# RMSNorm on one core: nineteen transfers of x and out joined into twelve, with whole-tile loads of the second and third tile

## The chip, the core and the metric

The kernel runs on one core of a Trainium2 chip. The metric is device time in microseconds (us) of one execution. The core has a matmul engine (TensorE, PE), three engines that matter here, VectorE (DVE), ScalarE (ACT) and GpSimd (POOL), and SyncE (SP), which in this kernel issues all transfers. The transfers themselves are carried out by 16 DMA engines.

## The reference

```python
batch, seq, dim = 16, 1024, 512          # x: float32, gamma: float32 [512]
eps = 1e-5
rms = np.sqrt(np.mean(x ** 2, axis=-1, keepdims=True) + eps)
return (x / rms * gamma).astype(np.float32)
```

x has 16,384 rows of 512 numbers, 33.55 MB, and out has as many. Every row is divided by its own root mean square and multiplied by gamma.

## The kernel before, in words

**Tiles and slots.** The rows are cut into four tiles of 128 partitions x 32 rows: partition p of a tile holds 32 rows that follow each other in memory, 64 KB. Three buffers, slot0 to slot2, hold tiles 0, 1 and 2, and tile 3 goes into slot0 once tile 0 has been stored. Everything is done in place: a slot is loaded, scaled and stored. A transfer names a range of rows, so that `load(0, 0, 8, 16)` brings rows 8 to 15 of tile 0 into slot0, for all 128 partitions (lines 44 to 50).

**Groups.** Compute runs over nine groups (lines 76 to 86). A group is (tile, first row, number of rows, pieces, share). For each group:
- `square_sums` (lines 89 to 99) goes over the pieces: ScalarE squares the rows of a piece into a scratch (line 96), VectorE sums each row (line 97). The scratch is PSUM for the first and third piece and a buffer for the second; a piece of 9 rows uses rows 23 to 31 of slot2 as its scratch, so these rows of slot2 can only be loaded once the last such piece has been summed.
- `inverse_rms` (lines 101 to 104): ScalarE takes the square root (line 102), VectorE the reciprocal (line 103).
- `scale_by_pool` (lines 106 to 113): GpSimd multiplies the last `share` rows by the reciprocal (line 109) and by gamma (line 110).
- `scale` (lines 115 to 118): ScalarE multiplies the other rows by the reciprocal, a row at a time (line 118), and `times_gamma` (line 122) lets VectorE multiply them by gamma, which stands in PSUM for it.

**Order.** The order on each engine is the order in which the program is written; nothing rearranges it. The main loop (from line 166) interleaves two groups: it issues the GpSimd part of group k, the squares of group k+1 (at most two pieces), half of ScalarE's scaling of group k, the third piece of squares of group k+1 if there is one, the rest of the scaling, VectorE's gamma product of group k, then the transfers that follow group k, and last the square root and reciprocal of group k+1. Engines run each through its own list and wait where they need another's result.

**Transfers.** SP issues all of them in program order. Those ahead of the loop (lines 52 to 61) are the first loads and gamma, which comes in pieces of a part of its 512 numbers; the others are issued by `transfers` (lines 129 to 149) after certain groups. An instruction of SP that waits holds up all that stand behind it. What the waits are: a load into a slot waits for the stores that read it and for compute that used it as scratch; a store waits for VectorE's and GpSimd's last product on its rows. There are also eight completion semaphores, taken in turn, so that the k-th transfer waits for the one eight before it.

In this text L0a and L0b are the loads of the first and second half of tile 0, L1, L2 those of tiles 1 and 2, L3a and L3b those of tile 3's halves; S0a, S0b, S1, S2, S3a and S3b are the stores.

Of the kernel before, what the change touches and what calls it, by code (L numbers as in the profile page):

```python
# [9 lines left out]
def kernel(  # L10
# [15 lines left out]
    N, D = xf.shape  # L26
# [17 lines left out]
    def load(t, slot, r0, r1):  # L44
        dma = nc.sync.dma_start(out=slots[slot][:, r0:r1], in_=xv[t][:, r0:r1])  # L45
        before_scale.append((slot, r0, r1, dma))

    def store(t, slot, r0, r1):
        dma = nc.sync.dma_start(out=ov[t][:, r0:r1], in_=slots[slot][:, r0:r1])
        before_scale.append((slot, r0, r1, dma))  # L50

    gamma_row = const.tile([1, D], fp32)
    pieces = (0, 128, 224, 320, 416, D)

    load(0, 0, 0, 1)
    load(0, 0, 1, 8)
    for c0, c1 in zip(pieces, pieces[1:]):
        nc.sync.dma_start(out=gamma_row[:, c0:c1], in_=gamma.unsqueeze(0)[:, c0:c1])
    load(0, 0, 8, 16)
    load(0, 0, 16, 32)  # L60
    load(1, 1, 0, 16)

    ones_col = const.tile([1, P], fp32)
    nc.gpsimd.memset(ones_col, 1.0)  # L64
# [9 lines left out]


    groups = [
        (0, 0, 7, (7,), 3),
        (0, 7, 9, (9,), 5),
        (0, 16, 16, (7, 9), 7),
        (1, 0, 16, (7, 9), 7),  # L80
        (1, 16, 16, (7, 5, 4), 7),
        (2, 0, 16, (7, 5, 4), 7),
        (2, 16, 16, (7, 5, 4), 7),
# [44 lines left out]

    def transfers(t, g):
        if (t, g) == (0, 0):  # L130
            store(0, 0, 0, 1)
            load(1, 1, 16, 32)
            store(0, 0, 1, 2)
            load(2, 2, 0, 23)
        elif (t, g) == (0, 16):
            store(0, 0, 2, 3)
            load(2, 2, 23, 32)
            store(0, 0, 3, 16)
            store(0, 0, 16, 32)
            load(3, 0, 0, 16)  # L140
            load(3, 0, 16, 32)
        elif (t, g) == (1, 16):
            store(1, 1, 0, 32)
        elif (t, g) == (2, 16):
            store(2, 2, 0, 32)
        elif (t, g) == (3, 0):
            store(3, 0, 0, 16)
        elif (t, g) == (3, 16):
            store(3, 0, 16, 32)
# [16 lines left out]
    for k, group in enumerate(groups):  # L166
        t, g, n, pieces, share = group
        mine = n - share
        half = (mine + 1) // 2
        ahead = groups[k + 1 :][:1]  # L170
        ss, todo = pieces_of(ahead[0]) if ahead else (None, [])
        scale_by_pool(rstd, t, g, n, share)
        for piece in todo[:2]:
            square_sums(*piece)
        scale(rstd, t, g, 0, half)
        for piece in todo[2:]:
            square_sums(*piece)
        scale(rstd, t, g, half, mine)
        times_gamma(t, g, 0, mine)
        transfers(t, g)  # L180
        for nxt in ahead:
            rstd = inverse_rms(ss, nxt[2])
# [30 lines left out]
```

## Time and profile before

| | |
|---|---|
| median of 3 runs | 161.59 us (161.41 to 161.67) |
| profiled execution: span from the first to the last instruction | 160.2 us; the runs' median is 1.4 us above it |
| VectorE busy | 112.0 us (70%), 39 instructions |
| ScalarE busy | 107.8 us (67%), 108 instructions |
| GpSimd busy | 106.4 us (66%), 24 instructions |
| TensorE busy | 2.0 us (1%), it only spreads gamma over the partitions |
| loads of x issued | 10: one of 256 KB, 1,792, 2,048, 2,304 and 5,888 KB, five of 4,096 KB |
| stores issued | 9: three of 256 KB, one of 3,328 KB, three of 4,096 KB and two of 8,192 KB |

How it is read: "busy" counts the time in which an engine carries out instructions, so a sum of shares over 100% is normal for engines that run side by side. The issue of a transfer on SP takes some 0.4 us there and is not counted as busy; the data move later, in the queue. A row of the timeline gives start and duration in us, the engine, the line of the kernel, the operation, what it writes and reads and its shape, and in brackets how long the engine was idle before and who released it. A row of the waits gives who waited for whom: us in total, how many times, the longest. "SPq" is SP's list of transfers. The page's row "DMA" gives the mean busy share of the 16 DMA engines in each of 40 equal slices of the span, in tenths.

### The profile page before, as it was taken

Reading aid. Unit: us, or ns where it says so; the run is one execution under the profiler, and the core shown is the slowest. Engines: PE = TensorE matmul, PEld = TensorE weight load, DVE = VectorE, ACT = ScalarE, POOL = GpSimd, SP = SyncE. Lnnn points to the kernel's source line nnn. Section 1 sums busy time; section 2 is a strip of 40 time slices with the busy share of each in tenths; the row PEclk is TensorE's granted clock in tenths of the full one; section 3 lists DMA queues with packets and bytes.
Section 4 is the critical chain, followed back from the end, with each engine's and each line's share of the span. In section 5 each row is a group of like instructions: output and inputs, shape, how many; then the busy total and the mean of one; then the engine's idle time right before and its main releaser. Section 6 shows DMA issues by size and latency. Waiting matters only on the chain.

```text
span 160.2 us, 276 instructions
## 1 busy us (share of the span) xinstructions
PE 2.0 (1%) x2; PEld 0.5 (0%) x2; DVE 112.0 (70%) x39; ACT 107.8 (67%) x108; POOL 106.4 (66%) x24
## 2 busy tenths in 40 slices
PE   0050000000000000000000000000000000000000
PEld 0010000000000000000000000000000000000000
DVE  0018098899798999999999999999999009700000
ACT  3071967976999998999899899989960990000000
POOL 1000951994999599999999999999999980000000
DMA  5999999899999899999999999996996996999994
GB/s 189 431 421 475 442 401 458 340 446 491 417 435 494 388 379 383 426 450 475 434 401 426 483 401 393 524 491 295 524 491 295 524 491 295 401 491 417 401 450 196
DMA packets 2747, 67.12 MB, mean 419 GB/s; under 512 B 313, under 2 KB 314, under 8 KB 826
## 3 DMA queue, kind: packets, MB, share of 16 engines
q1 hardware_dynamic: 2746, 67.11, 98.1%
q14 instruction: 1, 0.01, 0.0%
HBM read 33.56 MB, written 33.55 MB: 419 GB/s over the span
## 4 chain that ended last, share of the span: by engine, by line
DVE 59%; ACT 22%; DMA 4%; ACTq 0%; issue 0%; SPq 0%
DVE ss L97 36%; DVE slot L122 23%; ACT slot L118 8%; ACT slot L96 7%; ACT sq_psum L96 6%; DMA slot<-in_x_dram 4%; DVE ss L103 1%; ACT ss L102 1%; ACTq L208 0%; ACT gamma_b L165 0%; SPq L45 0%; ACTq L96 0%
## 5 line engine op out<-in xcount | busy, mean ns | idle before, releaser
L109 POOL TENSOR_TENSOR slot<-slot,ss 128x3584 f32<-128x3584 f32 (+2 forms) x9 | 47.0, 5218 | 24.1 <-DVE ss L103 24.1
L110 POOL TENSOR_TENSOR slot<-slot,gamma_b 128x3584 f32<-128x3584 f32 (+2 forms) x9 | 59.3, 6587 | 0.7
L97 DVE TENSOR_REDUCE ss<-sq_psum 128x7 f32<-128x3584 f32 (+1 forms) x13 | 42.2, 3247 | 13.7 <-ACT sq_psum L96 13.7
L118 ACT ACTIVATE slot<-slot,ss 128x512 f32<-128x512 f32 x75 | 47.3, 706 | 4.7 <-DVE ss L103 4.7
L122 DVE TENSOR_TENSOR slot<-slot,gamma_psum 128x4608 f32<-128x4608 f32 (+2 forms) x9 | 41.3, 4590 | 8.7 <-ACT slot L118 8.7
L96 ACT ACTIVATE sq_psum<-slot 128x3584 f32<-128x3584 f32 (+1 forms) x13 | 34.6, 2658 | 6.4 <-DMA slot<-in_x_dram 5.7
L97 DVE TENSOR_REDUCE ss<-slot 128x9 f32<-128x4608 f32 x3 | 14.9, 4954 | 4.4 <-ACT slot L96 4.2
L97 DVE TENSOR_REDUCE ss<-sq_sbuf 128x5 f32<-128x2560 f32 x5 | 14.0, 2803 | 0.0
L96 ACT ACTIVATE slot<-slot 128x4608 f32<-128x4608 f32 x3 | 12.1, 4033 | 0.0
L96 ACT ACTIVATE sq_sbuf<-slot 128x2560 f32<-128x2560 f32 x5 | 11.6, 2321 | 0.0
L102 ACT ACTIVATE ss<-ss,eps_t 128x16 f32<-128x16 f32 (+2 forms) x9 | 2.7, 305 | 11.9 <-DVE ss L97 11.9
L103 DVE RECIPROCAL ss<-ss 128x16 f32<-128x16 f32 (+2 forms) x9 | 2.1, 236 | 0.4 <-ACT ss L102 0.4
L66 PE MATMUL gamma_psum<-gamma_row,ones_col 1*128 1x512 f32 x2 | 2.0, 1122 | 8.6 <-DMA gamma_row<-in_gamma_dram 8.6
L72 ACT ACT_TABLE_LOAD x1 | 1.3, 1283 | 1.2 <-PEq L197 1.2
L165 ACT COPY gamma_b<-gamma_psum 128x512 f32<-128x512 f32 x1 | 0.6, 567 | 0.0
L66 PEld LDWEIGHTS gamma_psum<-gamma_row,ones_col 1*128 1x128 f32 x2 | 0.5, 308 | 8.6 <-issue 8.6
L64 POOL MEMSET ones_col<- 1x128 f32 x1 | 0.2, 195 | 0.3 <-POOLq L197 0.3
L197 POOL MEMSET const-float32-0.0<- 128x1 f32 x1 | 0.1, 99 | 0.2 <-issue 0.2
L72 ACT ACTIVATE table<-eps_t 128x1 f32<-128x1 f32 x1 | 0.2, 202 | 0.0
L197 POOL MEMSET const-bfloat16-1.0<- 128x1 bf16 x1 | 0.1, 102 | 0.0
L197 POOL MEMSET const-uint8-127<- 128x1 uint8 x1 | 0.1, 102 | 0.0
L197 POOL MEMSET const-float32-1.0<- 128x1 f32 x1 | 0.1, 99 | 0.0
(1 smaller groups left out, 0.1 us busy)
## 6 DMA issues: line engine op xcount, KB each, us to landing
slot<-in_x_dram SPq DMA_DIRECT2D x5, 4096.0 KB, 21.9
out_dram<-slot SPq DMA_DIRECT2D x3, 4096.0 KB, 23.4
slot<-in_x_dram SPq DMA_DIRECT2D x1, 5888.0 KB
out_dram<-slot SPq DMA_DIRECT2D x1, 3328.0 KB, 21.8
slot<-in_x_dram SPq DMA_DIRECT2D x1, 2304.0 KB, 14.3
slot<-in_x_dram SPq DMA_DIRECT2D x1, 2048.0 KB, 9.9
slot<-in_x_dram SPq DMA_DIRECT2D x1, 1792.0 KB, 7.0
out_dram<-slot SPq DMA_DIRECT2D x3, 256.0 KB
```

The costliest lines, as they stand in the source:

```text
L66: nc.tensor.matmul(gamma_psum[:, 0], ones_col, gamma_row, start=True, stop=True)
L72: nc.scalar.activation(out=table, in_=eps_t, func=AF.Sqrt)
L96: nc.scalar.activation(out=sq[:, :m], in_=rows, func=AF.Square)
L97: nc.vector.tensor_reduce(out=ss[:, r : r + m, 0], in_=sq[:, :m], axis=mybir.AxisListType.X, op=OP.add)
L102: nc.scalar.activation(out=ss[:, :n, 0], in_=ss[:, :n, 0], func=AF.Sqrt, bias=eps_t, scale=1.0 / D)
L103: nc.vector.reciprocal(out=ss[:, :n, 0], in_=ss[:, :n, 0])
L109: nc.gpsimd.tensor_tensor(out=part, in0=part, in1=by_row, op=OP.mult)
L110: last = nc.gpsimd.tensor_tensor(out=part, in0=part, in1=gamma_b.to_broadcast([P, share, D]), op=OP.mult)
L118: nc.scalar.activation(out=x[:, g + r, :], in_=x[:, g + r, :], func=AF.Copy, scale=rstd[:, r])
L122: scaled = nc.vector.tensor_tensor(out=part, in0=part, in1=gamma_psum.to_broadcast([P, r1 - r0, D]), op=OP.mult)
L165: nc.scalar.copy(out=gamma_b[:, 0], in_=gamma_psum[:, 0])
L197: nc = _bacc.Bacc("TRN2", target_bir_lowering=False, num_devices=1)
```

## The change

The first tile is loaded in two halves ahead of the loop instead of four pieces, tile 1 is loaded whole ahead of the loop, tile 2 is loaded whole after the first group, and the stores of single rows of tile 0 are gone: it is stored in two halves. Gamma comes in four pieces instead of five. The first group covers 16 rows instead of 7 and then 9, and the first group of tile 1 is squared in pieces of 7, 5 and 4 rows instead of 7 and 9. Because of this, pieces of 9 rows are left in tile 0 only. The loads ahead of the loop now wait for nothing; the load of tile 2 waits for the sum over the second piece of group (0, 16).

```diff
-    pieces = (0, 128, 224, 320, 416, D)
-
-    load(0, 0, 0, 1)
-    load(0, 0, 1, 8)
+    pieces = (0, 128, 256, 384, D)
+
+    load(0, 0, 0, 16)
     for c0, c1 in zip(pieces, pieces[1:]):
         nc.sync.dma_start(out=gamma_row[:, c0:c1], in_=gamma.unsqueeze(0)[:, c0:c1])
-    load(0, 0, 8, 16)
     load(0, 0, 16, 32)
-    load(1, 1, 0, 16)
+    load(1, 1, 0, 32)
...
     groups = [
-        (0, 0, 7, (7,), 3),
-        (0, 7, 9, (9,), 5),
+        (0, 0, 16, (7, 9), 7),
         (0, 16, 16, (7, 9), 7),
-        (1, 0, 16, (7, 9), 7),
+        (1, 0, 16, (7, 5, 4), 7),
...
         if (t, g) == (0, 0):
-            store(0, 0, 0, 1)
-            load(1, 1, 16, 32)
-            store(0, 0, 1, 2)
-            load(2, 2, 0, 23)
+            load(2, 2, 0, 32)
         elif (t, g) == (0, 16):
-            store(0, 0, 2, 3)
-            load(2, 2, 23, 32)
-            store(0, 0, 3, 16)
+            store(0, 0, 0, 16)
             store(0, 0, 16, 32)
             load(3, 0, 0, 16)
             load(3, 0, 16, 32)
```

In the changed kernel GpSimd has 7 of the first group's 16 rows, where it had 3 of 7 and 5 of 9.

## The prediction

> **What bounds the kernel now.** I read the page's head and its DMA rows first:
>
> ```profile
> span 160.2 us, 276 instructions
> ...
> DMA  5999999899999899999999999996996996999994
> ...
> q1 hardware_dynamic: 2746, 67.11, 98.1%
> HBM read 33.56 MB, written 33.55 MB: 419 GB/s over the span
> ```
>
> All of x and out, 67.1 MB, goes through one queue, whose packets occupy the 16 DMA engines for 98.1% of the span: 157.2 of 160.2 us. VectorE, the busiest compute engine, is at 70%. The chain of waits then seems to say the opposite, for it is made of VectorE and ScalarE. Its last row is the reason:
>
> ```profile
> 132.05 7.09 DVE slot L122
> ```
>
> The chain ends at 139.1 us, the last instruction that the profile calls work, while the last store is still 20 us from its end: the chain does not follow the queue. So I put the trace's packets in the order of their starts. Each engine takes one packet after another, and from the first packet (1.75 us) to the end of the last (158.99) none goes idle for more than 0.05 us after 8 us. The last packets of the first tile's second half, S1, S2 and the two last stores end at 81.4, 120.3, 139.6, 149.3 and 159.0 us. (S0a, L1 and so on: the first half's store of tile 0, the load of tile 1.) **The queue is the bound**; compute matters only where it hands SP a transfer too late. SyncE's timeline and waits show the hand-overs:
>
> ```profile
> 27.35 0.35 SPq L49 DMA_DIRECT2D out_dram<-slot  x1
> ...
> 28.69 0.43 SPq L45 DMA_DIRECT2D slot<-in_x_dram  x1
> ...
> 49.83 0.33 SPq L45 DMA_DIRECT2D slot<-in_x_dram  x1
> 50.25 5.48 SPq L49 DMA_DIRECT2D out_dram<-slot  x2
> 72.09 10.27 SPq L45 DMA_DIRECT2D slot<-in_x_dram  x2
> ```
>
> ```profile
> SPq L49 <- DVE slot L122: 56.1, 5, 26.0
> SPq L45 <- DMA out_dram<-slot: 25.7, 3, 13.7
> SPq L45 <- DVE ss L97: 20.1, 1, 20.1
> ```
>
> SP waits long, yet costs nothing, since every transfer is issued while the queue holds older ones. The first store is issued at 27.35 us, its packets start at 31.8.
>
> **The queue's own time, term by term.** A packet is one partition's share of a transfer, 8 per engine and transfer. In the trace a 32 KB packet takes 1.213 us and the next starts 1.2095 us after it; 64 KB: 2.418 and 2.414; 2 KB: 0.084 and 0.080. Two equations from the steps of 32 and 64 KB give 27.2 bytes per ns and about 4.5 ns for each packet. So 67.11 MB / 16 / 27.2 = 154.20 us, and 19 transfers x 8 x 4.5 ns = 0.68. By subtracting this work from the clock at several times I find the rest: first packets begin at 1.93 us on average and another 0.70 is lost by 8 us (first packets of 0.1 to 0.58 us in place of 0.084, then 14 KB packets of up to 0.82 in place of 0.535); three stalls, all while loads run, of 0.28 us at 29 to 32, 0.39 at 61 to 63, 0.23 at 99 to 101; about 0.01 per transfer for its semaphore packet; at the end 0.47 by which the last engine is behind the mean, and 1.17 until the span ends. Sum 154.88 + 1.93 + 0.70 + 0.90 + 0.1 + 0.47 + 1.17 = 160.15, the span. The median of the three runs, 161.59, is 1.4 above that; I carry differences over.
>
> **The change, part by part.**
>
> 1. *Nineteen transfers of x and out become twelve* (the diff replaces ten loads and nine stores by six and six). The bytes stay: 7 x 8 packets of 4.5 ns is 0.25 us less per engine, 7 semaphore packets 0.07. One gamma piece of 22 ns goes too, on one engine: nothing. **-0.32 us.** The nearest row against a larger price per transfer: between the single-row store and the loads on either side of it the steps are the same 0.08 and 1.21 us, with no gap.
>
> The Trainium skill (DMA: Bandwidth & Descriptors, Anatomy of one DMA, SWDGE path) fits 2.0 us of fixed time to a transfer; by it seven fewer would give 14 us. This queue hides it, as the gapless steps show.
>
> 2. *The start.* L0a is 32 KB packets instead of 2 and 14 KB. First-packet latency stays; engines that had used up their 2 KB packet waited up to 0.68 us for the next, which 1.2 us of work now covers. Bounds: all 0.70 gone, or half as much again lost, if cold memory and not the small packets slowed it. I take **-0.15**, near nothing, since the 14 KB packets were slow too.
>
> 3. *The stalls.* None falls into stores (excess there at most 0.02 us). Bounds: all 0.90 gone; or one more of the largest kind, +0.4. Two of the three precede a switch from loads to a large store, and one the first row store; the five switches from loads to stores become two. **-0.2.**
>
> 4. *Compute, at nothing, if it stays ahead.* The first square waits for L0a: L0a's last packet ends near 12.6 us (2.63 + 8 x 1.21 + skew), landing to ScalarE as now (7.90 to 8.31): start 13.0 instead of 8.31. Squares 3.1 + 4.0 run without a wait between; reduces (3.85, 4.95) end at 25.1, as now. Sqrt, reciprocal: GpSimd begins group (0,0) at 26.1 and needs 6.17 + 7.80. Squares of (0,16) 25.9 to 33.0, its second reduce ends at 38.0. **L2 waits for exactly this reduce** (its scratch is in slot 2; in before, too, the last rows' load is issued at 49.83, as the reduce ends at 49.80). SP is stuck there with S0a and S0b behind it; both come from later work. Issue at 38.05 plus the 1.0 us from issue to first packet (0.74 to 1.75): 39.1. The queue holds L0 and L1, 16.8 MB: 2.63 + 38.7 = 41.4. Margin 2.3 us. Next, L1 lands whole at 41.8; group (1,0) is squared 42.1 to 52.5 as 7, 5 and 4 rows (4.20 instead of 4.03 on ScalarE, 5.08 instead of 4.95 on VectorE), with nine scales of 0.706 between. Line 122 for (0,0) runs 38.7 to 43.7 and releases S0a; for (0,16) it ends at 60.0 (55.3 now), and the reciprocal of (1,0) at 60.3. From there GpSimd sets the pace, as it does now:
>
> ```profile
> 55.57 6.16 POOL L109 TENSOR_TENSOR slot<-slot,ss 128x3584 f32<-128x3584 f32 x1 [1.62 <-DVE ss L103]
> ...
> 97.56 6.17 POOL L109 TENSOR_TENSOR slot<-slot,ss 128x3584 f32<-128x3584 f32 x1
> 103.82 7.80 POOL L110 TENSOR_TENSOR slot<-slot,gamma_b 128x3584 f32<-128x3584 f32 x1
> ```
>
> 14.0 us per group, (2,16) ends at 111.6 now and at 60.3 + 4 x 14.0 = 116.3 then. Hand-overs after the change, issue against the time the queue would run dry: S0b 60.1 against 70.5, L3a 70.9 (S0a landed) against 80, L3b 80.6 against 90, S1 88.4 against 99.5, **S2 116.3 + 1.0 against 118.9 (first engine; 119.4 now), margin 1.6**, S3a 130.3 against 138, S3b 143.9 (139.2 + 4.7) against 148. All are in time, so the 4.7 us that compute loses costs **0**; without that cover, each us beyond a margin costs one.
>
> The Trainium skill (Perfetto Trace Analysis, DMA Optimizations, point 2) speaks against the change: splitting lets work start sooner when DMA engines are generally idle. By it joining the first pieces loses the 4.7 us; here the engines are at 98.1%, and the late start should stay hidden.
>
> Sum: -0.32 - 0.15 - 0.2 = **-0.67 us**: span 159.5, time 161.59 - 0.67 = **160.92**.
>
> **Rivals.**
> - *A late S2 (slower).* Its margin of 1.6 us is the smallest. Were (1,0) later than worked out by one 7-row reduce (3.85 us), all engines would stand idle 2.25 us between S1 and S2: 161.59 - 0.67 + 2.25 = 163.2. It decides for slower from 1.6 + 1.0 = 2.6 us late. For it: 18 us of chained work lie between L1's landing and GpSimd. Against it: each row repeats within 0.03 us, and the queue and the chain slip together if L1 is late. Chance 0.10; L2's hand-over, the same with 2.3, another 0.05 (about 162.5).
> - *Nothing measurable.* The merge saves its 0.25 to 0.32, but stalls and start remain or add: 161.3 to 161.8. For it: stalls may belong to time or memory. Chance 0.20. Here too belongs a change that does not do what it says: were 64 KB loads cut into smaller packets, the 0.25 would shrink; the stores of 64 KB are single packets now.
> - *Stalls gone.* With 0.9 and 0.5 saved instead: 161.59 - 0.32 - 0.9 - 0.5 = 159.9. Chance 0.07.
> - *The forecast*, 160.6 to 161.2: 0.58.
>
> About 0.2% (0.32 us) is what a measurement of this kernel can tell from no change. Forecast and vanished stalls, less a little of the forecast's edge, give faster 0.62; same 0.22; slower 0.16 (the late hand-overs and 0.01). The range, 160.2 to 162.3, leaves out most of the first rival and of the vanished stalls.
>
> **What would show it.** The queue's share stays near 98%, its packets fall by 7 x 128 plus semaphores to about 1,730; the mean rate rises to about 421 GB/s. First square at 13.0, L2 issued at 38 us, GpSimd's (1,0) at 60, S2 issued near 116, compute's end near 144. A DMA row with a slice well under 9 near 40 or 119 us would prove the first rival. A span above 160.2 with no dry spot would show my terms for start and stalls wrong.

## The result and the profile after

The changed kernel is a little slower: 162.11 us (median of 12 runs, 161.88 to 162.56) against 161.62 us for the kernel before (12 runs); the ratio is 1.0032, 95% interval 1.0022 to 1.0042. One of the 12 runs before took 163.90 us, in a slower state that this kernel falls into now and then, and is left out of the ratio. The forecast was 160.92, faster. The time lies in the stated range, but on the other side of no change.

The page's head, DMA row and queue rows of the changed kernel:

```profile
span 160.3 us, 255 instructions
...
DMA  7999999969969988999999999996996996999993
...
q1 hardware_dynamic: 1736, 67.11, 97.9%
...
HBM read 33.56 MB, written 33.55 MB: 419 GB/s over the span
```

The queue is the bound as before (98.1% then). It carries 1,010 packets fewer, and the mean rate is the same, where 421 GB/s was expected. The digits of the DMA row can't tell where time is lost: a packet that takes too long counts as busy. The bytes of a stretch can. Stretches of the changed kernel around the end of tile 2's load; after the bounds and the length come the busy time of PE, PEld, VectorE, ScalarE and GpSimd, then PEclk, the DMA share and GB/s:

```profile
48.20:57.87 9.67, 0.00 (x0) 0.00 (x0) 9.01 (x4) 9.67 (x12) 9.30 (x2) 1.00 1.00 434
57.87:61.30 3.43, 0.00 (x0) 0.00 (x0) 3.43 (x3) 3.43 (x5) 1.42 (x1) 1.00 1.01 306
61.30:70.90 9.60, 0.00 (x0) 0.00 (x0) 9.60 (x4) 8.68 (x11) 9.52 (x2) 1.00 1.01 437
```

The engines are fully occupied in all three (1.00, 1.01, 1.01), yet the middle one moves 306 GB/s in place of 434: 3.43 x (1 - 306/434) = 1.0 us is lost. Here all 16 engines carry the last 64 KB packet of tile 2's load, which takes 3.13 to 3.64 us in place of 2.418. The next packets are the first of S0a, the execution's first store, and take 1.213 us as ever.

SyncE's timeline of the changed kernel shows that no hand-over came late:

```profile
2.42 35.72 SPq L45 DMA_DIRECT2D slot<-in_x_dram  x3
43.39 16.66 SPq L49 DMA_DIRECT2D out_dram<-slot  x2
72.07 10.36 SPq L45 DMA_DIRECT2D slot<-in_x_dram  x2
87.95 55.91 SPq L49 DMA_DIRECT2D out_dram<-slot  x4
```

Each row is a group of issues from the first one's start to the last one's end: the issue of L2 ends at 38.14 us (the queue would have run dry at 41.4), that of the last store at 143.86 (needed at 148).

### The profile page after: what moved, and what is told of

Its sections match the earlier page's. It is cut to its first block, busy times and chain, and to the rows that moved or that the text cites. A ratio compares the mean times of both kernels' runs of the same rounds, so it can differ in the third digit from the quotient of the medians.

```text
span 160.3 us, 255 instructions
## 1 busy us (share of the span) xinstructions
PE 2.0 (1%) x2; PEld 0.5 (0%) x2; DVE 112.6 (70%) x38; ACT 108.3 (68%) x109; POOL 104.1 (65%) x22
## 4 chain that ended last, share of the span: by engine, by line
DVE 50%; DMA 24%; ACT 13%; SPq 1%; ACTq 0%; issue 0%
DVE ss L94 27%; DMA slot<-in_x_dram 24%; DVE slot L119 23%; ACT slot L115 8%; ACT sq_psum L93 3%; ACT sq_sbuf L93 1%; SPq L57 1%; DVE ss L100 1%; SPq L45 0%; ACTq L200 0%
## 5 line engine op out<-in xcount | busy, mean ns | idle before, releaser
L106 POOL TENSOR_TENSOR slot<-slot,ss 128x3584 f32<-128x3584 f32 (+1 forms) x8 | 45.9, 5733 | 30.9 <-DVE ss L100 30.9
L94 DVE TENSOR_REDUCE ss<-sq_psum 128x7 f32<-128x3584 f32 (+1 forms) x14 | 44.5, 3180 | 21.4 <-ACT sq_psum L93 21.4
L107 POOL TENSOR_TENSOR slot<-slot,gamma_b 128x3584 f32<-128x3584 f32 (+1 forms) x8 | 58.0, 7251 | 0.6
L119 DVE TENSOR_TENSOR slot<-slot,gamma_psum 128x4608 f32<-128x4608 f32 (+1 forms) x8 | 41.7, 5216 | 8.9 <-ACT slot L115 8.9
L94 DVE TENSOR_REDUCE ss<-sq_sbuf 128x5 f32<-128x2560 f32 x6 | 16.8, 2805 | 0.0
L93 ACT ACTIVATE sq_sbuf<-slot 128x2560 f32<-128x2560 f32 x6 | 13.9, 2320 | 0.0
L94 DVE TENSOR_REDUCE ss<-slot 128x9 f32<-128x4608 f32 x2 | 9.9, 4952 | 0.1
L93 ACT ACTIVATE slot<-slot 128x4608 f32<-128x4608 f32 x2 | 8.1, 4028 | 0.0
L99 ACT ACTIVATE ss<-ss,eps_t 128x16 f32<-128x16 f32 x8 | 2.4, 304 | 7.8 <-DVE ss L94 7.8
L100 DVE RECIPROCAL ss<-ss 128x16 f32<-128x16 f32 x8 | 2.0, 248 | 0.4 <-ACT ss L99 0.4
```

The costliest lines, as they stand in the source:

```text
L93: nc.scalar.activation(out=sq[:, :m], in_=rows, func=AF.Square)
L94: nc.vector.tensor_reduce(out=ss[:, r : r + m, 0], in_=sq[:, :m], axis=mybir.AxisListType.X, op=OP.add)
L99: nc.scalar.activation(out=ss[:, :n, 0], in_=ss[:, :n, 0], func=AF.Sqrt, bias=eps_t, scale=1.0 / D)
L100: nc.vector.reciprocal(out=ss[:, :n, 0], in_=ss[:, :n, 0])
L106: nc.gpsimd.tensor_tensor(out=part, in0=part, in1=by_row, op=OP.mult)
L107: last = nc.gpsimd.tensor_tensor(out=part, in0=part, in1=gamma_b.to_broadcast([P, share, D]), op=OP.mult)
```

## The experiments

In what follows a *stall* is queue time lost, worked out from the trace's packets as in the prediction: clock time less the work of the packets, bytes / 27.2 plus 4.5 ns each, mean over the 16 engines, of one profiled execution. The bounds chosen for a stretch move a stall by up to 0.08 us, and smaller ones stand as 0. The table holds all kernels. "Later" is ahead of the first large store, where smaller ones came first, or of the next large one (or at the time given); "tile 1" is the turn from tile 3's load to tile 1's store near 100 us.

| kernel | median us, ratio to the kernel before (95%) | first store: size, place | stall ahead of it | later | tile 1 |
|---|---|---|---|---|---|
| before | 161.62 | 1 row, 32 us | 0.27 | 0.36 | 0.22 |
| before, again | 161.63, 0.9999 (0.9986-1.0013) | 1 row, 32 us | 0.52 | 0.15 (42 us) | 0 |
| before, no row stores | 162.28, 1.0042 (1.0026-1.0059) | 16 rows, 61 us | 0.89 | 0 | 0.15 |
| before, one row store | 161.84, 1.0018 (1.0000-1.0037) | 1 row, 32 us | 0.34 | 0.32 | 0.17 |
| before, 1-2-4-9 rows | 162.10, 1.0030 (1.0018-1.0041) | 1 row, 32 us | 0.23 | 0.48 (42 us) | 0 |
| before, seven rows first | 162.76, 1.0070 (1.0041-1.0098) | 7 rows, 33 us | 1.15 | 0.04 | 0 |
| changed | 162.11, 1.0032 (1.0022-1.0042) | 16 rows, 61 us | 1.04 | 0 | 0.07 |
| changed, tile 2 in halves | 162.13, 1.0027 (1.0017-1.0037) | 16 rows, 61 us | 1.03 | 0 | 0.14 |
| changed, tiles 1 and 2 in halves | 162.37, 1.0033 (1.0008-1.0058) | 16 rows, 61 us | 1.00 | 0 | 0.15 |
| changed, one early row | 162.41, 1.0059 (1.0037-1.0081) | 1 row, 22 us | 0.21 | 0.72 | 0.09 |
| changed, four tiny stores | 162.50, 1.0068 (1.0044-1.0093) | 8 KB, 22 us | 0 | 1.02 | 0.06 |
| changed, two tiny stores | 162.14, 1.0036 (1.0022-1.0050) | 8 KB, 22 us | 0 | 0.98 | 0 |
| changed, one tiny store | 162.21, 1.0033 (1.0021-1.0045) | 8 KB, 51 us | 0 | 1.16 | 0.21 |
| changed, four tiny loads | 161.91, 1.0020 (1.0008-1.0032) | 16 rows, 61 us | 0.44 (and 0.23 earlier) | 0 | 0.20 |
| changed, early half store | 172.19 (2 runs) | 16 rows, 22 us | 1.25 | 0.29 | 0.07 |
| changed, tile 3 thrice | 201.03 (2 runs) | 16 rows, 61 us | 1.10 | 0 | 0 |
| changed, three row stores | 161.83, 1.0013 (1.0004-1.0022) | 1 row, 51 us | 0.24 | 0.14 | 0 |
| changed, S0a from ScalarE | 162.40, 1.0046 (1.0033-1.0060) | 16 rows, 54 us | 1.05 | 0 | 0.23 |

A stall belongs to one execution and the median to all, and the two should not be set against each other to a tenth: the profiled execution took 161.70 us with 1-2-4-9 rows, 161.54 with three row stores, 161.84 with two tiny stores and 161.87 with S0a from ScalarE, 0.3 to 0.5 below the medians. With four tiny stores it took 163.64, and its last engine ended 1.6 us behind the mean of the 16; in the other profiles that is 0.2 to 0.7 us.

**The kernel before, again.** No edit.

> The kernel before, unchanged, for a second profile of it. In the first one the queue lost 0.28 us just ahead of the first single-row store, 0.39 us at the end of tile 2's load ahead of the 13-row store, and 0.23 us at the end of tile 3's load. Theory A (the turn from loads to stores costs, and small early stores make it cheap): the first two stalls come back in the same places, 0.5 to 0.8 us together. Theory C (stalls belong to time or chance, and the changed kernel's 0.5 us lies outside the queue): stalls in other places or none. Time ratio 1.000 under all.

The time is the same, and the stall ahead of the first row store is back (0.52), the one ahead of the 13 rows is not. In its place 0.15 us is lost ahead of the second row store, at 42 us, where the first profile has nothing. Between two executions the shares vary, while the sum of the stalls up to the first large store is 0.63 and 0.67. That is A in part; this run alone does not exclude C. The profiled execution took 161.87 us with a span of 160.1, 1.8 more than the span; the changed kernel's took 162.05 with 160.3, 1.8 too. The first profile of the kernel before (span 160.2) thus was an execution of some 161.9 us, 0.3 above the median, and not 1.4 below it as I had read it: a run's time is 1.8 us more than its span.

**Without the row stores.** The three lines `store(0, 0, 0, 1)`, `store(0, 0, 1, 2)` and `store(0, 0, 2, 3)` are taken out of the kernel before.

```diff
-            store(0, 0, 3, 16)
+            store(0, 0, 0, 16)
```

> The kernel before without its three single-row stores: rows 0 to 15 of tile 0 are stored at once, everything else as before. Theory A: one stall of about 1 us ahead of the first large store at about 62 us in place of 0.28 and 0.39, three small transfers less (0.1 us): +0.2 to +0.5 us. Theory B (64 KB load packets make the stall long): here the load ahead of the store has packets of 36 KB (18 KB in each half), so the stall stays near 0.4 us and the time falls by 0.2 to 0.4 us. Theory C: no change beyond -0.1 us.

It is slower by 0.42% although it has three small transfers fewer, and has one stall of 0.89 us, ahead of its first large store (columns as above):

```profile
48.00:57.30 9.30, 0.00 (x0) 0.00 (x0) 8.74 (x4) 9.30 (x10) 7.69 (x2) 1.00 1.00 427
57.30:61.30 4.00, 0.00 (x0) 0.00 (x0) 4.00 (x2) 3.63 (x5) 4.00 (x1) 1.00 1.02 346
61.30:71.00 9.70, 0.00 (x0) 0.00 (x0) 9.70 (x5) 9.14 (x10) 9.62 (x3) 1.00 1.01 434
```

(4.0 x (1 - 346/434) = 0.8 us; these bounds cut through packets, so this is rougher than the 0.89.) By the medians this part alone, +0.66 us, brings all of the changed kernel's loss. Theories B and C give a faster kernel or none, and fall here; A stands.

**Tile 2 in halves.**

```diff
-            load(2, 2, 0, 32)
+            load(2, 2, 0, 16)
+            load(2, 2, 16, 32)
```

> The changed kernel with the load of tile 2 in two halves, issued one after the other in the same place: 32 KB packets in place of 64 KB ahead of the first store. Theory B: the stall of 1.07 us at 58 to 61 us shrinks to about half, time -0.5 us against the changed kernel (near the kernel before). Theory A: the stall stays about 1 us, time within 0.1 us of the changed kernel, +0.5 us against the kernel before.

The stall stays 1.03 us, now in the last two 32 KB packets of each engine: it is not the packet's size. Theory A.

**One early row.**

```diff
     load(0, 0, 16, 32)
+    nc.sync.dma_start(out=ov[0][:, 0:1], in_=slots[0][:, 0:1])
     load(1, 1, 0, 32)
```

> The changed kernel with one more transfer: row 0 of tile 0, as it was loaded, is stored to out between the loads of tile 0 and tile 1, and is overwritten by the ordinary store later. The extra bytes are the same as those of one single-row store, 0.64 us of queue time, not saved elsewhere. Theory A: a stall of about 0.3 us moves to the early store at 22 us, and that ahead of the first large store falls from 1.07 us to about 0.4: 0.64 + 0.3 - 0.67 = +0.3 us against the changed kernel. If all of the first turn's price is paid by the early store, whatever its size: 1 us at 22 us, none at 58, +0.64. If every turn to a large store costs the same: 1.07 us stays, +0.7 to +0.9. Theory B: 1.07 us stays at 58 us.

The stall splits, as A has it, but into 0.21 and 0.72 where A said 0.3 and 0.4. The time is +0.3 us against the changed kernel, A's figure, and that is luck: the extra row costs 0.64, the two stalls together, 0.93, are hardly less than 1.04, and it is the end of this profile that brings the time down again, where the last engine is 0.27 us behind the mean in place of 0.60. I took the pair for a sign that the stall grows with the time for which only loads have run (theory D): 0.07 to 0.2 after 20 us, 0.2 to 0.5 after 22 to 32, 0.72 after 38, 1.0 after 59. The next four runs went into that.

**Tiny stores and tiny loads.** `early` is a store of 512 bytes from each of 16 partitions, 8 KB; the first kernel has four of them between halves of loads, the second one at 51 us, the third four loads of that size into a spare buffer instead, the fourth two stores between whole loads.

```diff
+    def early(t, slot, r):
+        nc.sync.dma_start(out=ov[t][0:16, r, 0:128], in_=slots[slot][0:16, r, 0:128])
...
+    early(0, 0, 0)
+    load(1, 1, 0, 16)
+    early(0, 0, 16)
+    load(1, 1, 16, 32)
+    early(1, 1, 0)
...
+            load(2, 2, 0, 16)
+            early(1, 1, 16)
+            load(2, 2, 16, 32)
```

> The changed kernel with the loads of tiles 1 and 2 each in two halves and four stores of 512 bytes for 16 partitions (8 KB; rows as loaded, overwritten by the ordinary stores later) between the loads, so that a store stands in the queue about every 10 us: at 22, 32, 41 and 51 us, then the first large store at 61. Theory D (the stall ahead of a store grows with the time for which only loads have run: so far 0.1 to 0.2 us after 20, 0.3 to 0.5 after 32, 0.7 after 38, 1.0 after 59): nearly no stall at any of the five turns, at most 0.3 us in all in place of 1.04, some 0.2 us for more transfers, time 161.4 +- 0.2, faster than the changed kernel by 0.6 and than the kernel before by 0.1 to 0.3. Theory A1 (each engine pays about 1 us once, for its first stores, in parts by their size): tiny stores pay little and 0.7 to 1.0 us stays ahead of the first large store, time 162.1.

> The changed kernel with tile 2's load in two halves and one store of 8 KB between them, at 51 us, after 49 us of loads alone. Theory D: the tiny store meets nearly the whole stall (0.7 to 0.9 us at 49 to 51 us), the large store 10 us later almost none; time within 0.15 us of the changed kernel. Theory A1: the tiny store pays 0.1 to 0.3, the large one keeps 0.7.

> As the kernel with four tiny stores, with four loads of the same size (8 KB into a spare buffer) in their places. If the stores' direction is what shortens the stall (D and A1), nothing is gained here: 1.0 us ahead of the first large store, time 162.1 to 162.3. If it is only the cut of the loads or a small transfer between them, it is as fast as the one with stores.

> The changed kernel with two stores of 8 KB, at 22 and 41 us, between whole loads: three stretches of loads of about 20 us. Theory D: 0.1 to 0.3 us at each of the three turns, 0.5 in all, time 161.5 to 161.7. Theory A1: 0.7 to 1.0 ahead of the large store, time 162.1.

The tiny stores met no stall and spared none: 0.98 to 1.16 us remain ahead of S0a. Either they don't count for D or D is wrong; A1 had given them a small part, which isn't there either. The four tiny loads, meant as a control, gave 161.91 and a stall of 0.44, which none of the theories had expected.

**Two tests of D.** An extra store of 4 MB between tile 0's and tile 1's loads (rows as loaded, overwritten later), and tile 3's loads done three times over.

```diff
     load(0, 0, 16, 32)
+    nc.sync.dma_start(out=ov[0][:, 0:16], in_=slots[0][:, 0:16])
     load(1, 1, 0, 32)
```

```diff
-            load(3, 0, 0, 16)
-            load(3, 0, 16, 32)
+            for _ in range(3):
+                load(3, 0, 0, 16)
+                load(3, 0, 16, 32)
```

> The changed kernel with one more store of 4 MB (rows 0 to 15 of tile 0 as loaded, overwritten by the ordinary store later) between tile 0's loads and tile 1's: 9.7 us of queue time on top, so the time itself is near 172. What counts is the packets: a large store after 20 us of loads alone, then the ordinary first store after another 39 us of loads. Theory D (the stall grows with the time of loads alone since the last real store; 8 KB are too little to count as one): 0.1 to 0.2 us at 22 us, 0.6 to 0.8 at about 70 us. Theory A1 (about 1 us once, for the first large store of the execution): 0.9 to 1.1 at 22 us, at most 0.25 at 70 us.

> The changed kernel with the two loads of tile 3 repeated twice more (same data, same place): 38.8 us of queue time on top, so the time is near 200. The stretch of loads ahead of tile 1's store, 20 us in the changed kernel, with a stall of 0.07, becomes 58 us. Theory D: the stall there grows to about 1 us. Theory A1: it stays at 0.1 to 0.25 us. The stall ahead of the first store stays 1.0 under both.

Stretches of the kernel with the early half store, ahead of that store (columns as above):

```profile
9.50:19.20 9.70, 2.04 (x2) 0.50 (x2) 3.06 (x1) 6.25 (x2) 0.00 (x0) 1.00 1.00 433
19.20:22.90 3.70, 0.00 (x0) 0.00 (x0) 3.63 (x2) 0.87 (x1) 0.00 (x0) 1.00 0.98 283
```

After only 20 us of loads the first large store costs 3.7 x (1 - 283/433) = 1.3 us, and S0a, 39 us of loads later, 0.29 (a little over A1's bound, far from D's 0.6 to 0.8). And the kernel that loads tile 3 thrice, at its first store and ahead of tile 1's store, after 58 us of loads:

```profile
57.90:61.30 3.40, 0.00 (x0) 0.00 (x0) 3.40 (x3) 3.40 (x4) 1.30 (x1) 1.00 1.03 308
129.20:138.80 9.60, 0.00 (x0) 0.00 (x0) 5.18 (x2) 8.37 (x7) 0.00 (x0) 1.00 1.01 433
136.40:138.80 2.40, 0.00 (x0) 0.00 (x0) 2.40 (x2) 2.40 (x5) 0.00 (x0) 1.00 1.01 437
```

The last 2.4 us ahead of the store run at 437 GB/s: no stall. D falls twice over. What is left is A1: **the first large store of an execution, with nothing larger than 8 KB stored ahead of it, costs 0.89 to 1.25 us**, wherever it stands, in the load packets ahead of it (the kernel with tiny loads, 0.44, is the one exception); later turns from loads to stores cost 0 to 0.3.

**Seven rows first.** In the kernel before, all rows that are ready at 27 us go out in the first store.

```diff
-            store(0, 0, 0, 1)
+            store(0, 0, 0, 7)
             load(1, 1, 16, 32)
-            store(0, 0, 1, 2)
             load(2, 2, 0, 23)
...
-            store(0, 0, 2, 3)
             load(2, 2, 23, 32)
-            store(0, 0, 3, 16)
+            store(0, 0, 7, 16)
```

> The kernel before with the three single-row stores replaced by one store of the first seven rows (1.8 MB, 4.3 us of queue time) in the place of the first of them; the last nine rows of the half are stored where thirteen were. No byte more, two transfers fewer. Theory D: 0.3 to 0.5 us at the first store (32 us into loads), then 0.1 to 0.3 ahead of the nine rows (27 us of loads): time within 0.2 us of the kernel before. Theory A1: about 1 us at 32 us, near none later; 0.2 to 0.4 us slower than the kernel before.

A stall of 1.15 us at the first store and none later, +0.70%: A1 by place and stall; the time is above what either theory gave. In this profile the last three engines end 0.4 to 0.7 us behind the mean, where the very last ends 0.5 behind it in both profiles of the kernel before; that is part of it. A first store of one row cost 0.2 to 0.5, one of seven rows in the same place 1.15: between them its size decides.

**Tiles 1 and 2 in halves**, the control of the tiny loads: two more cuts as in "tile 2 in halves", nothing between.

> The changed kernel with tiles 1 and 2 each loaded in two halves and nothing between them: what the kernel with four tiny loads has without these. If that kernel's 161.9 us came from its cut loads: 161.9 here, with a stall of 0.4 to 0.7. If the cut of the loads does nothing, as it did for tile 2 alone: 162.1 to 162.2 and a stall of 1.0 us ahead of the first large store.

1.00 us of stall and 162.37: the cuts gain nothing, so it was something about the tiny loads, if anything: their median and their stall say so, but the two intervals overlap (1.0008 to 1.0032 and 1.0008 to 1.0058). I leave that open.

**Row stores put back, thinned out, grown, and S0a beside the loads.**

The first, in the changed kernel:

```diff
-            load(2, 2, 0, 32)
+            load(2, 2, 0, 16)
+            store(0, 0, 0, 1)
+            load(2, 2, 16, 24)
+            store(0, 0, 1, 2)
+            load(2, 2, 24, 32)
+            store(0, 0, 2, 3)
...
-            store(0, 0, 0, 16)
+            store(0, 0, 3, 16)
```

> The changed kernel with three single-row stores back, between pieces of tile 2's load (at 51, 56 and 61 us), the first half's other 13 rows after them. No byte more. Theory A2 (small first stores pay the first-store cost in small parts, less in sum than one large store does): 0.3 at 51 us, little at 56, 0.1 to 0.4 ahead of the 13 rows, sum 0.5 to 0.7 in place of 1.04, +0.15 us for four more transfers: 161.7 to 161.9, 0.2 to 0.4 below the changed kernel. If the row stores are not the cause: 162.2.

161.83 us, ratio 1.0013 (1.0004 to 1.0022), whose interval touches that of the changed kernel only at 1.0022; stalls of 0.24 and 0.14 in place of 1.04. With the run that takes the row stores out of the kernel before, this shows both ways that they, and not the early start or the cut loads, are what keeps that kernel's time down. It is still 0.2 us above the kernel before.

One row alone, in the kernel before: rows 1 and 2 go with the 13 others.

```diff
-            store(0, 0, 1, 2)
-            store(0, 0, 2, 3)
-            store(0, 0, 3, 16)
+            store(0, 0, 1, 16)
```

> The kernel before with the first of its single-row stores alone; the other two rows go with the 13. Theory A2 with one small store enough: time as before, 161.6. If each of the three takes a part, as the one early store in the changed kernel suggests (0.21 + 0.72 us): 0.3 at 32 us and 0.6 to 0.7 ahead of the 15 rows, 161.9 to 162.1.

161.84: by the medians one row store keeps two thirds of the 0.66 us that three keep (162.28 to 161.84 and to 161.62). The intervals are too wide to be sure of it (1.0000 to 1.0037 with one, 1.0026 to 1.0059 with none), and the stalls, 0.34 and 0.32, add up to no more than with three.

The growing stores, in the kernel before:

```diff
-            store(0, 0, 1, 2)
+            store(0, 0, 1, 3)
...
-            store(0, 0, 2, 3)
+            store(0, 0, 3, 7)
...
-            store(0, 0, 3, 16)
+            store(0, 0, 7, 16)
```

> The kernel before with its small stores grown from 1, 1, 1 and 13 rows to 1, 2, 4 and 9, in the same places. Same number of transfers, same bytes. If the size of each first store sets its share: the 4-row store ahead of tile 2's last rows pays 0.2 to 0.4 and the last none; sum 0.5 to 0.8, time 161.5 to 161.8. If growing steps train it without loss: sum 0.3, 161.3 to 161.4, faster than the kernel before.

162.10: slower than single rows. A stall of 0.48 us sits ahead of the second store, two rows at 42 us; the larger ones pass free. Of the expectation's first case only the sum came (0.71), not the place or the time, and of the second nothing: no faster version comes of it.

S0a from ScalarE, in the changed kernel (`before_scale` is given the transfer as `store` would):

```diff
-            store(0, 0, 0, 16)
+            dma = nc.scalar.dma_start(out=ov[0][:, 0:16], in_=slots[0][:, 0:16])
```

> The changed kernel with the first large store issued by ScalarE, after group (0,16)'s scaling at about 55 us, so that it runs beside the end of tile 2's load instead of behind it; tile 2 lands some 5 us later, near 66 us, before its first square needs it at 69. If the cost belongs to the queue's turn: other packets fill it and the stall goes, 161.0 to 161.3. If it belongs to the engines: about 1 us is lost in the load packets near 56 us all the same, 162.0 to 162.3.

The queue rows of this kernel from 50 to 72 us show that both queues ran at once:

```profile
q1 hardware_dynamic: 117, 5.41, 61.7%
q10 hardware_dynamic: 107, 3.51, 36.9%
```

The store was issued at 49.10 us, and its packets start at 54.26. Ahead of that, from 51 to 54 us, the load packets on q1 lose 1.05 us all the same: on each engine a 64 KB packet takes 3.31 to 3.69 us in place of 2.418. So the cost is not that of a turn within one queue.

## Why the prediction was wrong, point by point

**What bounds it: right.** The queue, with no dry spot. The span of 160.3 us without one is what the prediction had named as the sign that its terms for the start and the stalls are wrong.

**Nineteen transfers to twelve, -0.32: right in its main part.** The packets' work falls from 154.89 to 154.64 us, -0.25; the semaphore packets I did not separate.

**The start, -0.15: too much.** 2.62 us are lost by 9 us in both profiles of the kernel before, 2.57 in the changed one: -0.05. The small first packets had not been the reason: the first packets of 32 KB take 1.40 to 2.07 us in place of 1.213.

**The stalls, -0.2: this step failed.** I wrote that the five switches from loads to stores become two, and let each count alike. I had seen that two stalls preceded a switch to a large store and one the first row store, and then bounded the other side at +0.4 by "one more of the largest kind" among stalls that had been measured with small stores in front. The price was not one for each switch but one for the first real store, and the row stores that the change removes are what had kept it low: up to the first large store 0.63 and 0.67 us are lost with them, 0.89 and 1.04 without.

By the two first profiles the three stalls go from 0.85 to 1.11, +0.26 in place of -0.2. With -0.25 of work, -0.05 at the start and +0.13 at the end, where the last engine is 0.60 us behind the mean and not 0.47, that makes +0.09, and the spans are 160.2 and 160.3. The medians differ by more, 0.49: the first profile of the kernel before was an execution 0.3 above its median, and that of the changed kernel one 0.06 below. What is shorter in the median execution of the kernel before, no profile shows; that it is the stalls is likely from the two runs on the row stores, but not seen.

**Compute at nothing: right**, nearly to the number. First square 12.86 us (13.0 said); S2 issued at 115.94 (116.3), the first of the three stores in this row of SyncE:

```profile
115.94 27.91 SPq L49 DMA_DIRECT2D out_dram<-slot  x3
```

GpSimd in the changed kernel:

```profile
59.88 6.16 POOL L106 TENSOR_TENSOR slot<-slot,ss 128x3584 f32<-128x3584 f32 x1 [2.29 <-DVE ss L100]
...
101.88 6.16 POOL L106 TENSOR_TENSOR slot<-slot,ss 128x3584 f32<-128x3584 f32 x1
108.12 7.79 POOL L107 TENSOR_TENSOR slot<-slot,gamma_b 128x3584 f32<-128x3584 f32 x1
```

Group (1,0) starts at 59.88 (60.3 said) and (2,16) ends at 115.91; S2's packets start from 119.42 on, straight after S1's last. The compute path lost 4.3 us and the time did not see it. The rivals of a late S2 or L2 did not happen; the slower side was reached by the stalls, for which the forecast had kept 0.01 of the 0.16 that it gave to slower. That the time still lies in the range is luck: its upper part was there for the late hand-overs. "Nothing measurable", with stalls that remain or add, was the nearest rival, and its 161.8 fell 0.3 short.

## What to carry to other kernels

In a kernel that is bound by its transfers, compare packet durations with the same size's usual ones before merging transfers: a full DMA row hides lost microseconds, and the place where they are lost names what the small transfers were good for. Removing seven transfers saved 0.25 us of packet time here, less than what the three row stores among them were worth (0.66 us by the medians). And a disturbance seen only in one profile should be priced with its worst case, or looked at in a second profile, before a forecast of 0.4% is built on it.

## What the hardware showed that I had not expected

- The first store of some size costs all 16 engines about 1 us (0.98 to 1.25 in ten kernels, 0.89 in one, 0.44 with tiny loads between the loads), in the last load packets ahead of it: the last one of 64 KB, the last two of 32 KB, several of 18 KB. It does so at 22, 33, 54 and 61 us. Later turns cost at most 0.3 us after large stores, even after 58 us of loads.
- A store of 256 KB ahead pays 0.2 to 0.5 us itself and takes part of the price off the large one. The stalls up to the large store add up to 0.66 us with one row store, and to 0.63, 0.67 and 0.38 with three; least was gained by one raw row at 22 us (0.21 and 0.72). A store of 8 KB pays nothing and takes nothing off.
- What the engines do in that microsecond stays open. That stretches of loads build it up and that large load packets make it were tried and do not hold (1.03 us with 32 KB packets, 0.89 with 18 KB), and with the store on a queue of its own it came as well. That a part of out is written for the first time does not explain it either: in the changed kernel tile 1's store is the first to write its part, and the turn to it costs 0.07 us.
